# Padding three small SBUF tiles to 64 bytes, so that the tiles laid out behind them start elsewhere within 64 bytes

## The chip, the cores and the metric

The kernel runs on one core of a Trainium2 chip. The metric is the device time of one execution in microseconds. Before the change it is 2839.8 us, the median of three runs (2837.2, 2839.8 and 2843.13 us). One further execution was profiled; every row below comes from it.

## What is computed

Two blocks follow each other on 512 latent tokens of width 1024 (and 256 context tokens in the first block). All arithmetic is float32.

```python
x = ffn_sub(x, mod_lat[0:3], norm1_w, ffn1_w1, ffn1_w2)          # SwiGLU, 1024 -> 2*2816 -> 1024
s_ctx = ffn_sub(s_ctx, mod_ctx[0:3], norm1_w, ffn1_w1, ffn1_w2)
ctx_mix, lat_mix = parallel_mixer(h_ctx, h_lat, w_in, ...)       # HGRN2 and mLSTM heads
x = x + mod_lat[5] * lat_mix
x = ffn_sub(x, mod_lat[6:9], norm3_w, ffn2_w1, ffn2_w2)
# second block
y_ssm = _mamba2_mixer(...) @ w_ssm_out
y_nsa = _nsa_mixer(...) @ w_nsa_out
h = h + gate1 * ((sigmoid(hn @ w_gs) * y_ssm + sigmoid(hn @ w_ga) * y_nsa) @ w_o)
h = h + gate2 * _hier_moe(hn2, ...)                              # 32 experts, 2 per token
out = _rmsnorm(h, final_g)
```

`_hier_moe` sends each token to two of 32 experts; an expert is a SwiGLU of width 256.

## The kernel before, in words

**Dense products.** Every dense product (both FFNs, all input projections, the output projections) is done by `mm3` (lines 210 to 212). A float32 operand is split into a high and a low part of type fp32r, and three matmuls add up in PSUM: weights-high by features-high (L210), weights-high by features-low (L211), weights-low by features-high (L212). The stationary operand, which a weight load brings into the array ahead of each matmul, is a slice of 128 columns of `whi` or `wlo`; the moving operand is a slice of 512 columns (latent tokens) or 256 columns (context tokens, or half of the latent ones) of a feature tile. In one place, `proj_tok` (L555 to L557), the roles are turned round: 256 columns of `whi` or `wlo` move and 128 columns of the features are stationary. A psum tile takes 24 matmuls in a row (8 slices of the inner dimension by 3) in the projections and in the first layer of an FFN; in the second layer (`hh`, `hl` by the weights of `w2`) it takes 6 or 9. FFN 1 does latent and context tokens in turn, FFN 2 latent tokens alone.

**Feature tiles.** `lath`, `latl` (latent features, pool `hn`, used by almost every product up to 2360 us), `ctxh`, `ctxl` (context, pool `b1`), `hh`, `hl` (hidden layer of the FFN, pool `act`, opened anew for each FFN), `y0h`, `y0l`, `mh`, `mlo` (tail, pool `mo`), `y1h`, `y1l` (tail, pool `yy`). The experts read `ew` (weights, pool `ea`; here they move, as plain float32, and `xg` and `hT` are stationary), and L2176 and L2177 add each expert's rows up with `yhl` (pool `mo`) moving and `ohT` (pool `eb`) stationary, both fp32r.

**Where tiles lie.** Pools are stacked in SBUF. Those on the left are laid one behind the other in the order in which they are opened, from the low end: `cst` (constants), `hn`, `b1`, then the pools of each stage; `mo` is laid where `hn` was. Those on the right grow down from the high end: `tp` (nine tiles of 2048 bytes) and under it `wp` with `wraw`, `whi`, `wlo`. Within a pool tiles stand in the order of their first use, and each one's bytes per partition are rounded up to a multiple of 32. So a tile of four bytes takes 32, and moves all that lies behind it, in its pool and in the pools on top, by half of 64 bytes. The addresses that this gives in the program before, each as the rest after division by 64, and by 128:

| tile | role | rest by 64 | rest by 128 |
|---|---|---|---|
| `whi`, `wlo` (186,336 and on) | weights | 32 | 96 |
| `lath`, `latl` (21,504 and 37,888) | features | 0 | 0 |
| `ctxh`, `ctxl` | features | 0 | 0 |
| `hh`, `hl` of FFN 1 (125,120 and on) | features | 0 | 64 |
| `hh`, `hl` of FFN 2 (123,104 and on) | features | 32 | 96 |
| `y0h`, `y0l`, `y1h`, `y1l`, `mh`, `mlo` | features | 0 | 0 |
| `yhl` moving, `ohT` stationary | experts' sum | 0, 0 | 0, 64 |
| `ew` moving, `xg` stationary | experts | 0, 0 | 0, 0 |

Slices of a tile begin at multiples of 512 bytes further on, so every matmul of a tile has the rests of its tile.

**The three small tiles.** `eps` (L110, `setup`) holds 1e-6 for the norms and stands fourth in `cst`, ahead of everything else that is laid on the left. `inv` (L1133, `rope_tables`) holds the rope frequencies; it is allocated in pool `xq` while FFN 2 runs, and pool `act` of FFN 2 lies on top of `xq`. `frs` (L2240, `finish`) is the last tile of `mo`, and `yy`, `ea` and `eb` lie on top of `mo`.

**Order of the work.** Instructions are put in order by a scheduler at build time, with priorities that the code sets; weights come by DMA on SP's queue into `wraw` and are split by ScalarE (L191, `whi`) and VectorE (L192, `wlo`).

Of the kernel before, what the change touches and what calls it, by code (L numbers as in the profile page):

```python
# [10 lines left out]
F32 = mybir.dt.float32  # L11
# [29 lines left out]
class Kern:  # L41
# [60 lines left out]
    def setup(self):  # L102
        nc, cst = self.nc, self.cst
        self.ident = cst.tile([128, 128], F32, name="ident")
        nc.sync.dma_start(self.ident, self.i["k_ident"])
        self.ones = cst.tile([128, 128], F32, name="ones")
        nc.vector.memset(self.ones, 1.0)
        self.sel4 = cst.tile([128, 32], F32, name="sel4")
        nc.sync.dma_start(self.sel4, self.i["k_sel4"])
        self.eps = cst.tile([128, 1], F32, name="eps")  # L110
        nc.vector.memset(self.eps, 1e-6)
        self.tiny = cst.tile([128, 1], F32, name="tiny")
        nc.vector.memset(self.tiny, 7.8e-20)

# [1011 lines left out]
class Mix2:  # L1126
# [3 lines left out]
    def rope_tables(self, i, pool, cosd, sind):  # L1130

        nc = self.nc
        inv = pool.tile([128, 1], F32, name="inv")  # L1133
        nc.sync.dma_start(inv, i["k_invf"])
        pos = i["positions_2"][0]
        pf = self.tmp("posf")
        if pos.dtype == I32:
            raw = self.tmp("pos0").bitcast(I32)
            nc.sync.dma_start(raw[0:1, :], pos[None, :])
            nc.vector.tensor_copy(pf[0:1, :], raw[0:1, :])  # L1140
        else:
            p32 = pos.bitcast(I32)
            for r in range(2):
                raw = self.tmp("pos%d" % r).bitcast(I32)
                nc.sync.dma_start(raw[0:1, :], p32[r * 512:(r + 1) * 512][None, :])
                nc.vector.tensor_copy(pf[0:1, r * 256:(r + 1) * 256], raw[0:1, 0:512:2])
        p = self.pt("pb")
        nc.tensor.matmul(p, self.ones[0:1, :], pf[0:1, :], start=True, stop=True)
        ang = self.tmp("ang")
        nc.vector.tensor_scalar(ang, p, inv, None, op0=OP.mult)  # L1150
        MG = 12582912.0
        C1, C2, C3 = 6.28125, 1.9350051879882812e-03, 3.019916050561733e-07
        k = self.tmp("kk")
        nc.vector.tensor_scalar(k, ang, 1.0 / (2 * math.pi), MG, op0=OP.mult, op1=OP.add)
        nc.vector.tensor_scalar(k, k, MG, None, op0=OP.subtract)
        for c in (C1, C2, C3):
            nc.vector.scalar_tensor_tensor(ang, k, -c, ang, op0=OP.mult, op1=OP.add)

        ab = self.tmp("ab")
        nc.scalar.activation(ab, ang, AF.Abs)  # L1160
        s = self.tmp("sn")
        nc.vector.tensor_scalar(s, ab, -1.0, 3.14159274101257324, op0=OP.mult, op1=OP.add)
        nc.vector.scalar_tensor_tensor(s, s, -8.74227766e-08, ab, op0=OP.add, op1=OP.min)
        nc.scalar.activation(s, s, AF.Sin)
        sg = self.tmp("sg")
        nc.scalar.activation(sg, ang, AF.Sign)
        nc.vector.tensor_mul(s, s, sg)
        nc.sync.dma_start(sind, s)
        nc.vector.tensor_scalar(ab, ab, -1.0, math.pi / 2, op0=OP.mult, op1=OP.add)
        nc.scalar.activation(ab, ab, AF.Sin)  # L1170
        nc.sync.dma_start(cosd, ab)
# [786 lines left out]
class Moe:  # L1958
# [271 lines left out]
    def finish(self, mo, yac, yg, fg, out):  # L2230

        nc = self.nc
        ss = mo.tile([128, 4, 2], F32, name="fss")
        for c in range(4):
            for f in range(2):
                fs = slice(f * 512, f * 512 + 512)
                j = self.tmp("fj")
                nc.scalar.activation(j, yac[:, c, fs], AF.Square, accum_out=ss[:, c, f:f + 1])
                (nc.vector if f else nc.gpsimd).tensor_tensor(yg[:, c, fs], yac[:, c, fs], fg[:, fs], op=OP.mult)  # L2239
        r = mo.tile([128, 4], F32, name="frs")  # L2240
        nc.vector.tensor_add(r, ss[:, :, 0], ss[:, :, 1])
        nc.scalar.activation(r, r, AF.Ln, bias=self.eps, scale=1.0 / D)
        nc.scalar.activation(r, r, AF.Exp, scale=-0.5)
        for c in range(4):
            if c % 2:
                nc.scalar.activation(yg[:, c, :], yg[:, c, :], AF.Copy, scale=r[:, c:c + 1])
            else:
                nc.vector.tensor_scalar(yg[:, c, :], yg[:, c, :], r[:, c:c + 1], None, op0=OP.mult)
            nc.sync.dma_start(out[c * 128:(c + 1) * 128, :], yg[:, c, :])
# [326 lines left out]
```

## Time and profile before

| | us |
|---|---|
| median of three runs | 2839.8 |
| the profiled execution, its own time | 2847.28 |
| its span, first to last instruction | 2845.5 |
| TensorE matmuls busy | 2684.1 (94%) |
| TensorE weight loads busy (beside matmuls) | 2052.9 (72%) |
| VectorE, ScalarE, GpSimd busy | 1553.9, 995.2, 280.4 |

The span is what the engines took; 1.8 us lie around it. Busy time of a matmul runs from its issue to its modelled end, and matmuls overlap, so for a dense stream the distance from one start to the next tells more than the mean duration.

### The profile page before, as it was taken

What the parts mean: (1) busy time and instruction counts of PE and PEld (TensorE: products, weight loads), DVE (VectorE), ACT (ScalarE), POOL (GpSimd) and SP (SyncE); (2) the same over time, 40 slices, a digit from 0 to 9 for tenths busy, and PEclk for the clock granted to TensorE, in tenths of its full rate; (3) what the DMA queues carried; (4) which work ended last, traced back from release to release, by engine and by line L of the source; (5) the groups of instructions that cost most, each with busy time, mean ns of one, the idle gap of its engine ahead of it and who ended that gap; (6) DMA issues with size and microseconds to landing.
All of it is one profiled execution on the core that took longest, in us unless ns stands there. A gap on an engine that the chain in (4) does not pass through costs nothing. (4 is left out here: it accounts for less than half of the span.)

```text
span 2845.5 us, 40809 instructions
## 1 busy us (share of the span) xinstructions
PE 2684.1 (94%) x16161; PEld 2052.9 (72%) x16162; DVE 1553.9 (55%) x3022; ACT 995.2 (35%) x1787; POOL 280.4 (10%) x319
## 2 busy tenths in 40 slices
PE   7999999999998887999999899999999989969997
PEld 5788888888887765678788678777777767854443
DVE  6333333338367895554435756676666664454444
ACT  5211112225235663422223424555444443231112
POOL 2000000003001220100000101121122220000000
PEclk8999999999999998999999999999999999979999
DMA  7422222134333228732333433201234367269995
GB/s 261 149 89 67 59 61 66 46 97 118 94 102 103 64 83 263 260 96 82 105 95 103 135 87 95 80 13 43 78 104 119 97 195 242 74 245 377 379 378 203
DMA packets 340996, 384.66 MB, mean 135 GB/s; under 512 B 20793, under 2 KB 251581, under 8 KB 340546
## 3 DMA queue, kind: packets, MB, share of 16 engines
q1 hardware_dynamic: 338498, 373.62, 40.7%
q0 software_dynamic: 2304, 8.39, 0.8%
q8 instruction: 129, 2.11, 0.3%
q14 instruction: 65, 0.53, 0.1%
HBM read 352.33 MB, written 29.63 MB: 134 GB/s over the span
## 5 line engine op out<-in xcount | busy, mean ns | idle before, releaser
L191 ACT CAST whi<-wraw 128x1024 fp32r<-128x1024 f32 x277 | 285.9, 1042 | 756.7 <-PE pppa L211 329.3
L210 PE MATMUL pppa<-lath,whi 128*128 128x512 f32 (+4 forms) x1344 | 523.1, 390 | 19.5 <-ACT lath L1833 5.4
L211 PE MATMUL pppa<-latl,whi 128*128 128x512 f32 (+3 forms) x1344 | 519.7, 387 | 5.1 <-DVE latl L358 3.0
L212 PE MATMUL pppa<-lath,wlo 128*128 128x512 f32 (+3 forms) x1344 | 513.2, 384 | 0.0
L192 DVE TENSOR_TENSOR wlo<-wraw,whi 128x1024 fp32r<-128x1024 f32 (+1 forms) x273 | 332.4, 1224 | 252.0 <-ACT whi L191 247.4
L210 PEld LDWEIGHTS pppa<-lath,whi 128*128 128x128 f32 (+3 forms) x1344 | 253.0, 188 | 87.4 <-ACT whi L191 11.9
L211 PEld LDWEIGHTS pppa<-latl,whi 128*128 128x128 f32 (+2 forms) x1344 | 252.6, 188 | 65.4 <-DVE latl L358 5.4
L212 PEld LDWEIGHTS pppa<-lath,wlo 128*128 128x128 f32 (+2 forms) x1344 | 252.1, 188 | 55.5 <-issue 2.5
L211 PE MATMUL pppb<-hl,whi 128*128 128x512 f32 (+1 forms) x576 | 195.3, 341 | 0.0
L210 PE MATMUL pppb<-hh,whi 128*128 128x512 f32 (+1 forms) x576 | 193.1, 344 | 0.0
L212 PE MATMUL pppb<-hh,wlo 128*128 128x512 f32 (+1 forms) x576 | 191.5, 341 | 0.0
L416 DVE SCALAR_TENSOR_TENSOR xT<-pppb,sG,xT 128x512 f32<-128x512 f32 (+1 forms) x144 | 96.7, 689 | 137.7 <-PE pppb L212 137.5
L396 DVE TENSOR_TENSOR hf<-sg,pppa 128x256 f32<-128x256 f32 (+1 forms) x68 | 39.7, 584 | 234.6 <-PE pppa L212 233.3
L210 PE MATMUL pppf<-lath,whi 128*128 128x512 f32 x320 | 128.9, 403 | 5.9 <-ACT lath L1833 2.2
L210 PE MATMUL pppa<-ctxh,whi 128*128 128x256 f32 (+1 forms) x440 | 125.1, 284 | 7.9 <-DVE W L919 7.9
L211 PE MATMUL pppf<-latl,whi 128*128 128x512 f32 x320 | 128.3, 401 | 0.8 <-DVE latl L1834 0.7
L2137 PE MATMUL pppa<-ew,xg 128*64 128x512 f32 x512 | 128.3, 607 | 0.0
L212 PE MATMUL pppf<-lath,wlo 128*128 128x512 f32 x320 | 127.4, 398 | 0.6 <-DVE wlo L192 0.6
L210 PEld LDWEIGHTS pppb<-hh,whi 128*128 128x128 f32 x576 | 108.0, 188 | 27.6 <-issue 5.8
L211 PE MATMUL pppa<-ctxl,whi 128*128 128x256 f32 (+1 forms) x440 | 124.6, 283 | 0.3 <-POOL ctxl L356 0.3
L212 PE MATMUL pppa<-ctxh,wlo 128*128 128x256 f32 (+1 forms) x440 | 124.7, 284 | 0.0
L211 PEld LDWEIGHTS pppb<-hl,whi 128*128 128x128 f32 x576 | 108.4, 188 | 16.1 <-issue 3.4
(697 smaller groups left out, 4999.6 us busy)
## 6 DMA issues: line engine op xcount, KB each, us to landing
wraw<-in_ffn_w_dram SPq DMA_DIRECT2D x132, 512.0 KB, 3.9
wraw<-in_w_in_dram SPq DMA_DIRECT2D x102, 512.0 KB, 4.0
ew<-in_w_exp_gate_dram SPq DMA_DIRECT2D x64, 512.0 KB, 8.0
ew<-in_w_exp_up_dram SPq DMA_DIRECT2D x64, 512.0 KB, 4.6
ew<-in_w_exp_down_dram SPq DMA_DIRECT2D x32, 1024.0 KB, 10.6
mraw<-in_w_mod_dram SPq DMA_DIRECT2D x40, 512.0 KB, 6.5
wraw<-in_w_mod_dram SPq DMA_DIRECT2D x32, 512.0 KB, 3.9
mraw<-in_w_ada_dram SPq DMA_DIRECT2D x32, 512.0 KB, 5.8
```

What stands on the lines that cost most here:

```text
L191: nc.scalar.copy(hi[:, :n], raw[:, :n])
L192: (nc.gpsimd if pool else nc.vector).tensor_sub(lo[:, :n], raw[:, :n], hi[:, :n].bitcast(F32))
L210: nc.tensor.matmul(out, wh, xh, start=start, stop=False)
L211: nc.tensor.matmul(out, wh, xl, start=False, stop=False)
L212: nc.tensor.matmul(out, wl, xh, start=False, stop=stop)
L396: nc.vector.tensor_mul(h[:, :n], sg[:, :n], pp[1])
L416: nc.vector.scalar_tensor_tensor(x[:, o, :], p[:, :n], gate[:, o:o + 1], x[:, o, :], op0=OP.mult, op1=OP.add)
L2137: nc.tensor.matmul(ph[x * 64:x * 64 + 64, :], xg[:, k, x * 64:x * 64 + 64], wts[k // 4 * 2 + x][:, :, k % 4, :], start=(k == 0), stop=(k = ...
```

## The change

Three tiles become 64 bytes wide, and the code uses the part of them that it used before. No operand, loop or instruction is otherwise touched; the one memset of `eps` covers 16 columns in place of 1.

```diff
-        self.eps = cst.tile([128, 1], F32, name="eps")
-        nc.vector.memset(self.eps, 1e-6)
+
+        eps = cst.tile([128, 16], F32, name="eps")
+        nc.vector.memset(eps, 1e-6)
+        self.eps = eps[:, :1]
...
-        inv = pool.tile([128, 1], F32, name="inv")
+        inv = pool.tile([128, 16], F32, name="inv")[:, :1]
...
-        r = mo.tile([128, 4], F32, name="frs")
+        r = mo.tile([128, 16], F32, name="frs")[:, :4]
```

## Rows read from the trace of the kernel before

**Rows 1.** The page: span, and each engine's busy time, share and instructions
```profile
span 2845.5 us, 40809 instructions
PE 2684.1 (94%) x16161; PEld 2052.9 (72%) x16162; DVE 1553.9 (55%) x3022; ACT 995.2 (35%) x1787; POOL 280.4 (10%) x319
```
**Rows 2.** Busy time by stretch, FFN 1 and FFN 2; PEclk is the granted clock
```profile
core 0: us, PE busy (x) PEld busy (x) DVE busy (x) ACT busy (x) POOL busy (x), PEclk, DMA share, GB/s
100.00:700.00 600.00, 595.19 (x3472) 501.05 (x3467) 246.71 (x390) 146.75 (x232) 21.95 (x27) 1.00 0.26 80
1200.00:1580.00 380.00, 370.98 (x1677) 295.75 (x1676) 172.51 (x228) 105.99 (x145) 7.10 (x11) 0.99 0.33 99
```
**Rows 3.** Timeline of PE, 512 columns: `y1h` and `y1l`, first matmul and the next stream's
```profile
2384.07 0.39 PE L210 MATMUL pppa<-y1h,whi 128*128 128x512 f32 x1
...
2406.47 0.39 PE L210 MATMUL pppa<-y0h,whi 128*128 128x512 f32 x1
```
**Rows 4.** Timeline of PE, 512 columns: `hh` and `hl` of FFN 2
```profile
1284.74 0.40 PE L210 MATMUL pppb<-hh,whi 128*128 128x512 f32 x1
...
1286.36 0.39 PE L211 MATMUL pppb<-hl,whi 128*128 128x512 f32 x1
1286.59 0.39 PE L212 MATMUL pppb<-hh,wlo 128*128 128x512 f32 x1
...
1300.87 0.39 PE L212 MATMUL pppb<-hh,wlo 128*128 128x512 f32 x1
```
**Rows 5.** Timeline of PE, 512 columns: `yhl` by `ohT`
```profile
2583.66 0.39 PE L2177 MATMUL pppb<-yhl,ohT 128*128 128x512 f32 x1
...
2586.93 0.39 PE L2177 MATMUL pppb<-yhl,ohT 128*128 128x512 f32 x1
```
**Rows 6.** Timeline of PE, 256 columns: context, turned round, FFN 2
```profile
144.83 0.28 PE L210 MATMUL pppa<-ctxh,whi 128*128 128x256 f32 x1
...
150.08 0.28 PE L210 MATMUL pppa<-ctxh,whi 128*128 128x256 f32 x1
...
730.27 0.28 PE L555 MATMUL pppa<-whi,lath 128*128 128x256 f32 x1
...
730.98 0.28 PE L555 MATMUL pppa<-whi,lath 128*128 128x256 f32 x1
...
1537.36 0.28 PE L210 MATMUL pppb<-hh,whi 128*128 128x256 f32 x1
...
1538.80 0.28 PE L210 MATMUL pppb<-hh,whi 128*128 128x256 f32 x1
```
**Rows 7.** Groups by line and shape: how many matmuls; mean ns is the modelled duration
```profile
L210 PE MATMUL pppa<-lath,whi 128*128 128x512 f32 x1160 | 467.8, 404 | 16.2 <-ACT lath L1833 5.4 <-ACT lath L1105 5.0 <-ACT whi L191 4.8
L210 PE MATMUL pppf<-lath,whi 128*128 128x512 f32 x320 | 128.9, 403 | 5.9 <-ACT lath L1833 2.2 <-ACT whi L191 1.7 <-DVE mth L1852 1.1
...
L210 PE MATMUL pppa<-ctxh,whi 128*128 128x256 f32 x432 | 122.8, 284 | 7.9 <-DVE W L919 7.9
...
L555 PE MATMUL pppa<-whi,lath 128*128 128x256 f32 x192 | 54.9, 289 | 0.0
```
**Rows 8.** The same groups within 60 to 680 us: the second layer of FFN 1
```profile
L210 PE MATMUL pppb<-hh,whi 128*128 128x256 f32 x224 | 62.2, 284 | 0.0
L210 PE MATMUL pppb<-hh,whi 128*128 128x512 f32 x152 | 61.3, 403 | 0.0
```
**Rows 9.** Groups of plain float32 matmuls: in NSA, in SSD, the experts'
```profile
L2137 PE MATMUL pppa<-ew,xg 128*64 128x512 f32 x512 | 128.3, 607 | 0.0
...
L1452 PE MATMUL pppa<-PT,vt 128*64 128x128 f32 x640 | 60.3, 283 | 0.3 <-DVE PT L1434 0.3
...
L1751 PE MATMUL pppa<-W,xt 128*64 128x128 f32 x256 | 23.8, 285 | 0.0
```
**Rows 10.** DMA issues of 512 KB: KB each, median us to landing
```profile
wraw<-in_ffn_w_dram SPq DMA_DIRECT2D x132, 512.0 KB, 3.9
...
mraw<-in_w_mod_dram SPq DMA_DIRECT2D x40, 512.0 KB, 6.5
```

## The prediction

> **What bounds the kernel now.** The page comes first: TensorE is busy for 94% of the span, VectorE for 55%, ScalarE for 35% [rows 1]. [...] A modelled duration (403 ns) overlaps the next matmul, so I read the pace from the timeline, as the distance between starts.
>
> There the reader sees two paces for matmuls of the same shape. The tail's `y1h` and `y1l` take 96 matmuls of 512 columns from 2384.07 to 2406.47 us: 22.40 / 96 = 233.3 ns each [rows 3]. The second layer of FFN 2 takes 63 (21 times three) from 1286.59 to 1300.87: 14.28 / 63 = 226.7 ns [rows 4]. Both streams have a new weight load for every matmul and no idle time. What differs is where the moving tile begins: weights at rest 32 in both, `y1` at 0, `hh` of FFN 2 at 32, so that only here features and weights stand at the same place. The fast pace isn't there at once: the first seven of that stream, from 1284.74 to 1286.36, take 1.62 / 7 = 231.4 ns, and then it locks in [rows 4].
>
> At 256 columns the order is the other way round. Context products (0 against 32) take 45 matmuls in 5.25 us, 116.7 ns each; products turned round (weights moving at 32, features loaded at 0) 0.71 / 6 = 118.3; FFN 2 with both at 32 takes 12 in 1.44 us, 120.0 ns [rows 6]. Standing at the same place costs 3.3 ns there.
>
> **What the change does, part by part.** `eps` goes from 4 to 64 bytes, rounded 32 to 64: all behind it on the left moves up by 32, `lath`, `latl`, `ctxh`, `ctxl`, FFN 1's `hh` and `hl`, `mh` and `y0` among them, from rest 0 to rest 32. `whi` and `wlo` hang from the high end and stay. `inv` adds 32 under pool `act` of FFN 2, 64 in all, which keeps its `hh` at rest 32 by 64 (123,104 becomes 123,168; by 128 it goes from 96 to 32, a point I come back to). `frs` adds 32 above `mo`, so `yy`, `ea` and `eb` move by 64 and keep their rests: `y1` stays at 0 against 32. No instruction is added; the memset of `eps` has 15 columns more before the first product, where all wait for the first loads, and I price it at nothing.
>
> *512 columns.* `lath` and `latl` have 1160 + 320 matmuls on each of three lines [rows 7], 4440; FFN 1's second layer 152 on each [rows 8], 456. Together 4896, each 233.3 - 226.7 = 6.6 ns faster once locked: -32.3 us. Lock-in takes some back: seven matmuls at 231.4 in place of 226.7 are 33 ns a stream. If every 24 matmuls began anew, 4896 / 24 = 204 streams would give back 6.7 us; many run longer (63 in rows 4 alone), so I take 4.5. That leaves -27.8 us.
>
> *256 columns.* Context: 432 on each of three lines [rows 7], 1296 by 3.3 ns, +4.3 us. The products turned round: 192 on three lines [rows 7], 576 by 120.0 - 118.3, +1.0 us. FFN 1's second layer has 672 [rows 8], in short streams between the 512-column ones; I take nothing, and +2.2 us as the upper end. Smaller groups of both widths on `lath`, `y0` and `mh` have both signs and are left out.
>
> *Experts.* `xg`, stationary, moves to 32 and `ew`, moving, stays at 0; `yhl` moves to 32 against `ohT` at 0. Plain float32 matmuls don't show the place: `PT` by `vt`, both at 0, 283 ns; `W` by `xt`, both at 32, 285 [rows 9]. So nothing for `xg`. From both sides: its 512 matmuls run in pairs, and 256 times 6.6 ns is 1.7 us either way.
>
> *Transfers and other engines.* `mraw`, `xT` and the rows that the experts gather now land at rest 32. `wraw` stands there already and lands 512 KB in 3.9 us, `mraw` at 0 in 6.5 [rows 10]: nothing to pay. VectorE and ScalarE, which split the weights and make `hh` and `hl`, are busy for 246.71 and 146.75 of FFN 1's 600 us [rows 2], so matmuls 3% faster still leave them cover; next late would be the split weights, at the first matmul of a stream.
>
> *Sum.* -27.8 + 4.3 + 1.0 = -22.5 us. In the FFNs 98.6% of the time is TensorE's (966.17 of 980), so I take 22 us. The profiled execution took 2847.3 us in all, which becomes 2825; it is 7.5 us over the median of the runs, 2839.8, from which 22 us leave 2818 us.
>
> **Rivals.**
>
> *128 bytes decide, not 64.* Against the forecast stands one stream: `yhl` by `ohT`, both at rest 0 by 64, takes 3.27 / 14 = 233.6 ns [rows 5], the slow pace, though moving and stationary stand at the same place within 64. By 128 they are 64 apart, while FFN 2's fast stream has 96 and 96. If the distance counts within 128, the change takes `lath` from 0 to 32 against 96, still apart: no gain. FFN 1's `hh` goes from 64 to 96 and meets the weights, but in streams of six to nine, which end as the lock begins; FFN 2's `hh` goes from 96 to 32 and loses: 152 on three lines there too, 456 by 6.6 ns, +3.0 us. About 2842 us. For the forecast speak two things: in `yhl`'s case both are at 0, while the only fast stream has both at 32, and a start halfway into 64 bytes may be what is needed; and the stream of `yhl` is short, 15 matmuls in these rows.
>
> *Slower: the 256-column price without the 512-column gain.* If 64 bytes are enough for the pace of 120.0 ns, but 226.7 needs 128, then context and turned products pay 5.3 us, FFN 2's second layer 3.0 us, FFN 1's 256-column part up to 2.2: 2839.8 + 8 to 10, about 2849 us. It decides as soon as `ctxh` runs at 120 and `lath` stays at 233. Against it: in FFN 2 both appear together.
>
> *The place plays no part.* FFN 2's stream could be fast for another reason, for instance that one weight tile serves it and no 256-column matmul comes between. Then nothing moves: 2840 us. Against it: `y1` has no 256-column neighbours either, and is slow [rows 3, 4]. [...]
>
> **How the numbers follow.** The forecast gets 0.52, 128 bytes 0.28, no part 0.06, slower 0.14. The first is all faster: its best end has no lock-in and no 256-column price (2839.8 - 32.3 = 2807.5), its worst 6.7 us of lock-in, 7.5 us of 256-column price (2822). The second and third are within 0.2% (5.7 us, about what a measurement of this kernel can tell from no change), the fourth beyond. Faster 0.52, same 0.34, slower 0.14. The likeliest case alone ranges from 2807 to 2824; the range given, 2807 to 2845, takes in the two cases without change as well and leaves out the slower one. The predicted time is that of the likeliest, 2818.
>
> **What would show it.** In the timeline of the changed kernel, `lath` in FFN 2 should start every 226.7 to 228 ns in long streams, with some seven slower ones at each start, `ctxh` every 120, `y1` still every 233.3, and FFN 2's `hh` still every 226.7. If `lath` stays at 233 and FFN 2's `hh` falls back to 233, 128 bytes decide; if `ctxh` goes to 120 and `lath` does not follow, the slower rival. If all paces are as forecast and the time isn't, the waits for `whi` and for `hf` in the FFNs have taken the gain. Paces other than these two on `lath` would make the whole argument wrong.

## The result and the profile after

The changed kernel takes 2822.8 us (median of five runs, 2818.4 to 2827.2) where the kernel before takes 2843.1 (median of five, 2837.2 to 2847.9): ratio 0.9924, 95% interval 0.9903 to 0.9944. That is 20.3 us less by the medians. The forecast was 22 us less, and 2818 us. The total came close to the forecast; the paces it was built from did not, and most of this document is about that.

The page after: the span is 25.3 us shorter and TensorE's busy time 24.6 us, with the same number of instructions; the other engines are where they were [rows 1].

```profile
span 2820.2 us, 40809 instructions
PE 2659.5 (94%) x16161; PEld 2052.4 (73%) x16162; DVE 1552.7 (55%) x3022; ACT 994.8 (35%) x1787; POOL 276.4 (10%) x319
```

Busy time by stretch, FFN 1 and FFN 2: both stretches are as full as before, but more matmuls fit into them, 3516 for 3472 and 1745 for 1677 [rows 2] (the second stretch now also catches more of what follows FFN 2). The granted clock is the same, 1.00 and 0.99.

```profile
core 0: us, PE busy (x) PEld busy (x) DVE busy (x) ACT busy (x) POOL busy (x), PEclk, DMA share, GB/s
100.00:700.00 600.00, 595.14 (x3516) 508.60 (x3515) 250.89 (x391) 146.83 (x233) 21.92 (x27) 1.00 0.26 80
1200.00:1580.00 380.00, 371.87 (x1745) 302.56 (x1744) 181.56 (x242) 109.84 (x153) 13.78 (x19) 0.99 0.33 101
```

The timeline of TensorE, first and last rows of six streams. In order: 48 context matmuls (to the first `hh` behind them), 96 of products turned round (to the first `ctxh`), 96 later ones of the same shape, 141 on `lath` and `latl` in FFN 2, the 72 on `hh` and `hl` that follow, and 96 on `y1`.

```profile
141.27 0.28 PE L212 MATMUL pppa<-ctxh,whi 128*128 128x256 f32 x1
...
146.92 0.39 PE L212 MATMUL pppb<-hh,whi 128*128 128x512 f32 x1
...
689.37 0.28 PE L557 MATMUL pppa<-whi,lath 128*128 128x256 f32 x1
...
700.28 0.28 PE L557 MATMUL pppa<-whi,ctxh 128*128 128x256 f32 x1
...
739.79 0.28 PE L557 MATMUL pppa<-whi,lath 128*128 128x256 f32 x1
...
751.10 0.28 PE L557 MATMUL pppa<-whi,ctxh 128*128 128x256 f32 x1
...
1289.74 0.40 PE L213 MATMUL pppa<-latl,whi 128*128 128x512 f32 x1
...
1322.03 0.39 PE L212 MATMUL pppb<-hh,whi 128*128 128x512 f32 x1
...
1338.51 0.39 PE L212 MATMUL pppa<-lath,whi 128*128 128x512 f32 x1
...
2360.40 0.40 PE L212 MATMUL pppa<-y1h,whi 128*128 128x512 f32 x1
...
2382.81 0.39 PE L212 MATMUL pppa<-y0h,whi 128*128 128x512 f32 x1
```

The distance between starts, divided by the count: context 5.65 / 48 = 117.7 ns (116.7 in rows 6, not the 120 of the forecast); turned round 10.91 / 96 = 113.6 in one stream and 11.31 / 96 = 117.8 in another (118.3 in rows 6); `lath` 32.29 / 141 = **229.0**, a pace that no row of before has; `hh` of FFN 2 16.48 / 72 = 228.9 (227.2 over its whole first stream before, 16.13 / 71 from the first of rows 4 to the last); `y1` 22.41 / 96 = 233.4, unchanged [rows 3]. The same stream of `lath` before, from the same place in FFN 2:

```profile
1302.15 0.39 PE L211 MATMUL pppa<-latl,whi 128*128 128x512 f32 x1
...
1335.04 0.40 PE L210 MATMUL pppb<-hh,whi 128*128 128x512 f32 x1
```

32.89 / 141 = 233.3 ns. So one matmul on `lath` became 4.3 ns cheaper, not 6.6.

To add this up over the kernel, I take for every kind of stream the mean distance between starts (gaps over 300 ns, or 160 at 256 columns, left out) and multiply its difference to before by the number of matmuls. I call this **the account** below.

| stream (matmuls) | before, ns | after, ns | us |
|---|---|---|---|
| `lath`, 512 columns (4464) | 233.5 | 229.5 | -17.6 |
| FFN 1's `hh`, 512 columns (456) | 233.0 | 230.6 | -1.1 |
| products turned round, 256 (768, context included) | 118.3 | 115.0 | -2.5 |
| `y0` and `y1` (384) | 233.3 | 231.4 | -0.7 |
| context, 256 (1320) | 116.9 | 117.2 | +0.3 |
| FFN 2's `hh`, 512 columns (456) | 227.5 | 228.9 | +0.6 |
| smaller groups (`hh` and `lath` at 256, `mh`, `yhl`) | | | -1.1 |

Together -22.1 us, of 25.3 by the spans and 20.3 by the medians. Here nothing has to be sought beyond the matmuls' pace; the question is what sets it.

### The profile page after: what moved, and what is told of

It is laid out like the page before. It is cut to its first block, busy times and chain, and to the rows that moved or that the text cites. A ratio compares the mean times of both kernels' runs of the same rounds, so it can differ in the third digit from the quotient of the medians.

```text
span 2820.2 us, 40809 instructions
## 1 busy us (share of the span) xinstructions
PE 2659.5 (94%) x16161; PEld 2052.4 (73%) x16162; DVE 1552.7 (55%) x3022; ACT 994.8 (35%) x1787; POOL 276.4 (10%) x319
## 5 line engine op out<-in xcount | busy, mean ns | idle before, releaser
L398 DVE TENSOR_TENSOR hf<-sg,pppa 128x256 f32<-128x256 f32 (+1 forms) x68 | 39.7, 584 | 228.6 <-PE pppa L214 227.2
```

The source lines that it names most:

```text
L398: nc.vector.tensor_mul(h[:, :n], sg[:, :n], pp[1])
```

## The experiments

All places below are rests by 256, and a **distance** is how far the features stand past the weights by 256. From the addresses in front: weights 224; before, `lath`, `ctxh`, `y0`, `y1` 0 (distance 32), FFN 1's `hh` 192 (224), FFN 2's `hh` 224 (0). In the changed kernel the distance is 64 for `lath`, `ctxh` and `y0`, 0 for FFN 1's `hh`, 64 for FFN 2's and 96 for `y1`. In products turned round the weights move, so the distance counts the other way: 224 before, 192 after. Every ratio and difference is to the kernel before on the same chip, whose median was 2842.2 us beside the three kernels with another `eps`, 2845.7 beside the two with the weights moved, and 2841.9 beside the last three.

**Streams run alone.** A kernel of its own, with one stream per pair of places; 26 pairs at 512 and at 256 columns. Its inner part (`REPS` is 4):

```python
for rep in range(REPS):
    for k in range(8):
        s = slice(wo + (k % 8) * 128, wo + (k % 8) * 128 + 128)
        for q, v in enumerate((vh, vl, vh)):
            nc.tensor.matmul(p[:, :n], w[:, s], v[:, mo:mo + n],
                             start=(rep == 0 and k == 0 and q == 0), stop=(rep == REPS - 1 and k == 7 and q == 2))
```

> This kernel leaves out the whole model: it only runs streams of 96 fp32r matmuls of 512 columns, then the same of 256 columns, each matmul with a fresh weight load, nothing else beside them. The letter behind m says where the moving operand begins, the letter behind w where the weights do, as the rest after division by 256 in steps of 16 bytes (A 0, B 16, C 32, D 48, E 64, G 96, H 112, I 128, K 160, O 224). Theory 1, the distance within 128 bytes decides: at 512 columns AA, CC, EE, GG 226.7 ns a matmul, the pairs 64 apart (AE, CG, EA, GC) 229.6 as lath shows it now at 32 by 96, all pairs 32 or 96 apart 233.3; AI, GO, CK like AA, GG, CC; at 256 columns 120.0 on the diagonal and 117 elsewhere. Theory 2, it is where the moving tile begins: columns mC and mG fast (226.7 to 229.6) whatever the weights, mA and mE 233.3. Theory 3, the place plays no part: all 26 streams of a width within 0.5 ns of each other.

The timeline: the weights stand at 32 (`wC`), the features at 0, 32, 64 and 96; each row is the first of 96 matmuls, the last row the first of the next case.

```profile
97.18 0.40 PE L40 MATMUL nmAwC<-vh,w 128*128 128x512 f32 x1
...
119.57 0.40 PE L40 MATMUL nmCwC<-vh,w 128*128 128x512 f32 x1
...
141.34 0.40 PE L40 MATMUL nmEwC<-vh,w 128*128 128x512 f32 x1
...
163.74 0.40 PE L40 MATMUL nmGwC<-vh,w 128*128 128x512 f32 x1
...
185.72 0.39 PE L40 MATMUL nmAwE<-vh,w 128*128 128x512 f32 x1
```

22.39, 21.77, 22.40 and 21.98 us by 96: 233.2, 226.8, 233.3 and 229.0 ns. Beside them VectorE only copies each stream's result, 25 copies of 17.28 us in all, and busy time by stretch shows a granted clock of 1.00 with TensorE busy for 575.00 of 575 us:

```profile
11.00:586.00 575.00, 575.00 (x2485) 466.54 (x2484) 17.28 (x25) 0.00 (x0) 0.00 (x0) 1.00 0.00 1
```

So the place plays a part (theory 3 falls), it isn't where the features alone begin (theory 2 falls: `mC` is fast against `wC` and slow against `wA`, `wE` and `wG`), and the distance counts. But not by 128 as theory 1 had it (the first letter is the features' place, the second the weights'): `AI`, `CK` and `OG`, equal by 128 and 128 apart by 256, take 232.3 to 232.4 and not 226.7, and 64 past is fast (`EA`, `GC` 229) where 64 short is slow (`AE`, `CG` 233.3). By 256 every stream whose two operands begin at multiples of 32, as tiles do, fits one row (means over the second half of each stream):

| distance by 256 | 512 columns, ns | 256 columns, ns |
|---|---|---|
| 0 | 226.7 | 120.0 |
| 32 | 233.3 | 117.8 |
| 64 | 228.9 | 117.8 |
| 96 | 233.3 | 120.0 |
| 128 | 232.4 (one 233.3) | 118.7 |
| 160 | 234.2 | 118.6 |
| 192 | 233.3 | 113.3 (`AE`), 117.8 (`CG`) |
| 224 | 233.3 | 118.3 |

The changed kernel's `lath`, FFN 2's `hh` and `y1` are rows 64, 64 and 96 of this table, those of the kernel before rows 32, 0 and 32; `yhl` by `ohT` [rows 5] is row 192. Weights that begin at an odd multiple of 16 don't fit: at distance 0 `BB` has 233.3, `DD` 230.0 and `HH` 231.1, and `CD`, 16 short, has 226.7.

**eps alone.** The other two pads as in the kernel before; the edit is to the changed kernel.

```diff
-        inv = pool.tile([128, 16], F32, name="inv")[:, :1]
+        inv = pool.tile([128, 1], F32, name="inv")[:, :1]
...
-        r = mo.tile([128, 16], F32, name="frs")[:, :4]
+        r = mo.tile([128, 4], F32, name="frs")[:, :4]
```

> Only eps is widened; inv and frs stay as in the kernel before. lath, ctxh, y0, mh and FFN 1's hh stand where the change puts them, FFN 2's hh goes to 0 by 96, y1 to 32 by 96. Theory 1 (eps alone carries the gain, through lath's place): lath at 512 columns 229.6 ns, y1 229.6 in place of 233.4, FFN 2's hh 233 in place of 228.9 (456 by 4 ns, +2 us), FFN 2's 256 columns 117; about 2823 to 2826 us, ratio to the kernel before 0.992 to 0.994. Theory 2 (the gain hangs on all three pads): less than half of it is left, over 2832 us.

2826.0 us, ratio 0.9946 (0.9929 to 0.9962). `lath` 229.6 and `y1` 228.9 (distance 64), FFN 2's `hh` 233.1 (distance 32). The account gives -21.8 us where the medians give -16.2. The paces and the time are those of theory 1: `eps` carries the gain. By the account, of the other two pads, `inv` is worth 1.9 us (`hh` of FFN 2 at 64 in place of 32), and `frs` costs 1 (`y1` at 96 in place of 64).

**eps wider still.** All that the change moves by 32 moves by 64, or by 96.

```diff
-        eps = cst.tile([128, 16], F32, name="eps")
+        eps = cst.tile([128, 24], F32, name="eps")
```

> eps widened to 96 bytes in place of 64, so that all that the change moves by 32 moves by 64; inv and frs as in the change. lath, ctxh and y0 stand at 64 by 96, FFN 1's hh at 0, FFN 2's hh at 64, y1 at 96. Theory 1 (distance within 128: 32 apart is slow, from which side ever): lath 233.3 ns, ctxh 116.9, FFN 2's hh 233.3, y1 226.7 with its lock-in; 2843 us plus 2 for FFN 2's hh less 1 for y1, ratio 0.999 to 1.002. Theory 2 (any move away from the old place helps, or the moved transfers and other engines' tiles bring the gain): about as the change, 2823 us, ratio 0.992. Theory 3 (distance counted one way only, 96 minus 64 = 32 being nearer than 96 minus 0): in between, lath about 229 to 231.

2853.5 us, ratio 1.0051 (1.0033 to 1.007): slower than before. `lath` 233.6, FFN 2's `hh` 233.3, and `ctxh` goes from 116.9 to 119.9, which alone is +3.8 us; the account is +7.8 us, of 11.3 by the medians. Distance 96 has the high price in both columns of the table, 233.3 and 120.0 ns. Theory 1 had the paces of `lath` and of FFN 2's `hh` right; those of `ctxh`, of `y1` (226.7 expected, 233.3 measured, at distance 128) and the time it had wrong, since 96 and 32 are not the same distance. Theory 2, that any move helps or that moved transfers bring the gain, falls.

```diff
-        eps = cst.tile([128, 16], F32, name="eps")
+        eps = cst.tile([128, 32], F32, name="eps")
```

> eps widened to 128 bytes, so that all that the change moves by 32 moves by 96; inv and frs as in the change. lath, ctxh, y0, mh, FFN 2's hh stand at 96 by 96, the place of the weights by 128 as well as by 64; FFN 1's hh at 32, y1 at 0. Theory 1 (distance within 128; 0 apart gives the full pace at 512 columns and costs at 256): lath 226.7 to 227.5 ns (4464 by 2 to 3 ns below the change, -10 to -13 us), ctxh 120.0 in place of 117.2 (1308 by 2.8, +3.7 us), products turned round 120 in place of 115 (768 by 5, +3.8 us), lath at 256 columns 480 by 3, +1.5 us; net -2 to -5 us against the change, 2818 to 2821 us, ratio 0.991 to 0.992. [...] Theory 3 (lock-in never comes in streams of 24): lath 230 or more, 2828 to 2832 us.

2850.6 us, ratio 1.0029 (1.0014 to 1.0044). This was the test of "the same place by 64 and by 128", 96 and 96, and none of the theories had the time (only theory 3's "230 or more" fits `lath`'s pace). The timeline of the same stream on `lath`:

```profile
1304.63 0.39 PE L213 MATMUL pppa<-latl,whi 128*128 128x512 f32 x1
...
1337.53 0.40 PE L212 MATMUL pppb<-hh,whi 128*128 128x512 f32 x1
```

32.90 / 141 = 233.3 ns; other streams of it have 232.4, the mean is 232.8. By 256 features and weights are 128 apart, and 232.4 is what that row of the table has. The account is +1.1 us; what the other 7 us of the median are isn't shown.

**The weights moved, the features left.** If the distance decides, it can be had from either side. Kernel before, with one pad on the right that takes the weights down to 0:

```diff
         nc.vector.memset(self.tiny, 7.8e-20)
+        pw = self.tp.tile([128, 56], F32, name="pw")
+        nc.vector.memset(pw, 0.0)
```

> The kernel before with eps, inv and frs as they were; the weights move instead: a pad of 224 bytes among the temporaries on the right takes whi and wlo from rest 224 to rest 0 by 256, where lath, ctxh, y0, y1 and mh stand all along. Theory 1 (the distance from weights to features by 256 decides, with the paces of the streams run alone: 0 apart 226.7 and 120.0 ns, 32 apart 233.3 and 117.8, 32 short 233.3 and 118.3): lath at 512 columns 227 ns (4452 by 6.7, -30 us), y0, y1 and mh 504 by 6.7, -3.4 us; against it ctxh 120 (1302 by 3.1, +4.0), products turned round 120 (768 by 1.7, +1.3), lath at 256 columns +1.0, FFN 2's hh 233.3 in place of 227.5 (456, +2.6); FFN 1's hh 233 as before and 113 to 118 at 256 columns (-0.5 to -3.6 us). Net -25 to -28 us, ratio to the kernel before 0.990 to 0.991. Theory 2 (it is where the features themselves begin, not the distance): lath, y0 and y1 stay at 233.3, ratio 0.999 to 1.001. Theory 3 (128 bytes, as in the forecast's rival): same paces as theory 1 for lath, but FFN 2's hh at 96 by 0 and FFN 1's at 64 by 0 like lath at 96 and 64 by 0; the streams run alone speak against it.

2824.9 us, ratio 0.9928 (0.99 to 0.9955), with every feature tile where it was before. The timeline, context and `lath` streams as above:

```profile
143.76 0.28 PE L212 MATMUL pppa<-ctxh,whi 128*128 128x256 f32 x1
...
149.51 0.40 PE L212 MATMUL pppb<-hh,whi 128*128 128x512 f32 x1
...
1299.57 0.40 PE L213 MATMUL pppa<-latl,whi 128*128 128x512 f32 x1
...
1331.59 0.40 PE L212 MATMUL pppb<-hh,whi 128*128 128x512 f32 x1
```

`lath` 32.02 / 141 = 227.1, `ctxh` 5.75 / 48 = 119.8, `y1` 226.7, FFN 2's `hh` (now at distance 224) 233.3: as the table has it, for both widths. Here the forecast's own numbers appear, 6.6 ns less at 512 columns and 3 more at 256. Over the whole kernel `lath` has 227.9 (-24.7 us) and context +3.6, turned round +1.2, FFN 2's `hh` +2.7; the account is -21.4 us, near the measured 20.8. The expected 25 to 28 was too much by the start of each stream: about 300 of some 4200 gaps on `lath` are still 231 or 236 ns, nearly all among the first twelve of a stream, and behind the twelfth the mean is 226.7.

**Each stream at its best.** Three pads more than in the run before: `ctxh` at distance 64, FFN 1's `hh` at 192, FFN 2's at 0.

```diff
                     lat = [hp.tile([128, 8, L], F32R, name="lat" + x) for x in "hl"]
+                    pc = hp.tile([128, 16], F32, name="pc")
+                    self.nc.vector.memset(pc, 0.0)
...
+                ph = self.act.tile([128, 48], F32, name="ph")
+                nc.vector.memset(ph, 0.0)
...
-        inv = pool.tile([128, 1], F32, name="inv")
+        inv = pool.tile([128, 64], F32, name="inv")[:, :1]
```

> As the run before, with three pads more, so that each stream stands where the streams run alone were fastest: 64 bytes behind lath take ctxh and ctxl to 64 past the weights, 192 bytes keep FFN 1's hh at 64 short of them, inv of 256 bytes puts FFN 2's hh at the weights' own place. Theory 1: lath at 512 columns 227 ns, ctxh 117 in place of 120 (-3.7 us against the run before), context products turned round 114 to 118 (-0.5), FFN 2's hh 227.5 (-2.6) and 120 at 256 columns (+0.4); 31 to 34 us below the kernel before, ratio 0.988 to 0.989, and 10 to 14 us below the changed kernel. Theory 2 (faster matmuls now run into another wait, for split weights or loads): paces as said, ratio 0.992 or more, with idle time of TensorE in the FFNs in place of the gain.

2818.5 us, ratio 0.9902 (0.9879 to 0.9925), the lowest median of all versions. `lath` 228.0, `ctxh` 117.7, FFN 2's `hh` 226.8, FFN 1's `hh` at 256 columns 115.7 (118.6 before); the account is -27.1, the measurement -27.2 us. So no wait took the gain (theory 2 falls); the expected 31 to 34 was again too much by the start of streams.

**Streams run alone, finer.** The first kernel with weights at 224 and distances in steps of 16, and with three questions more: the stream ahead, the load's width (`cols`), and distances past 256. Two lines of it:

```python
s = slice(wo + k * 128, wo + k * 128 + cols)
...
nc.tensor.matmul(p[:cols, :n], w[:, s], v[:, mo:mo + n],
```

> This kernel leaves out the whole model, as the first one with streams alone. Weights stand at 224 by 256, as in the kernel; n and h are streams of 96 matmuls of 512 and 256 columns, with the distance of the features past the weights in bytes (0 to 240 in steps of 16); x0 to x13 are 256 columns at distances 0, 64, 0, 192, 32, 64, 32, 192, 64, 192, 128, 64, 128, 192 in turn; c64 and c32 have weight loads of 64 and 32 columns in place of 128 at distances 0, 32, 64, 128; ta to tj are streams of 24 that alternate widths; p256, p288, p512 are distances past 256 at 512 columns. Theory 1 (distance by 256 decides): n000 226.7, n032 233.3, n064 228.9, n096 233.3, n128 232.4, n160 234.2, n192 and n224 233.3; h000 120.0, h032 and h064 117.8, h128 118.7; h192 113.3 or 117.8; p256 and p512 as n000, p288 as n032; x of one distance alike up to two states at 64 and 192 that the start of the stream picks. If the extra time over the columns is what a weight load takes from the moving stream: c64 and c32 nearer to each other and to the bare columns, c32 below 225 ns at every distance and the spread between distances a quarter of that with 128. Theory 2 (the load's width plays no part, the place costs per matmul): c32 as n of the same distance. Theory 3 (absolute place): n differs from the first streams of the same distance.

At 512 columns the distances 0 to 224 in steps of 32 repeat the table: 226.7, 233.3, 228.9, 233.3, 232.4, 234.3, 233.3, 233.3. A whole 256 past is as fast as 0 (226.7 in its second half), and 288 as slow as 32 (233.3). At 256 columns 192 gives 113.3 in all five long streams, whatever ran ahead of them at that width, but 117.6 and 117.7 in two short ones behind 512 columns; 160 gives 117.3 here and 118.6 in the first kernel, 32 gives 116.7 for 117.8, so at 256 columns the distance isn't all (theory 3 in part). The widths of the loads: the rows are the first of 96 matmuls with loads of 32 columns at distance 0, and the last of them, which shares its row (x2) with the first at distance 32.

```profile
790.13 0.39 PE L43 MATMUL c32d<-vh,w 128*32 128x512 f32 x1
...
812.14 0.63 PE L43 MATMUL c32d<-vh,w 128*32 128x512 f32 x2
```

22.01 / 95 = 231.7 ns at distance 0, where loads of 128 columns give 226.7; at distance 32 the stream has 233.1, as with 128. Loads of 64 columns give 230.0 and 231.0. At distances 64 and 128 loads of 64 columns give 228.6 and 229.4, loads of 32 give 231.7 and 230.9 (128: 228.9 and 232.4). Neither theory holds: a narrower load shrinks the spread between the distances from 7 ns to some 2, but to the middle (64 columns) or the slow end (32), and the fastest of these eight streams has 228.6. What part the load has therefore stays open; a stream with fewer loads than matmuls, which would tell whether the loads are behind it at all, wasn't run.

**The features moved back by 32.** `eps` and `tiny` share a tile, all on the left falls to 224, the weights' place, with less memory than before.

```diff
-        self.eps = cst.tile([128, 1], F32, name="eps")
+        et = cst.tile([128, 2], F32, name="eps")
+        self.eps, self.tiny = et[:, :1], et[:, 1:]
         nc.vector.memset(self.eps, 1e-6)
-        self.tiny = cst.tile([128, 1], F32, name="tiny")
```

> The kernel before, but eps and tiny share one tile, so that everything behind them on the left moves back by 32: lath, ctxh, y0, y1 and mh go from 0 to 224 by 256, the place of the weights, which stay; FFN 1's hh goes to 160 (64 short of the weights), FFN 2's to 192 (32 short). Every distance is the one of the run with the weights moved, reached from the other side and with 32 bytes less of memory. Theory 1 (the distance by 256 decides): paces and time as in that run: lath 228 ns, ctxh 120, FFN 2's hh 233, 2822 to 2827 us, ratio 0.991 to 0.994. Theory 2 (the absolute place has a part too): lath's pace off 228 by over 1 ns.

2828.1 us, ratio 0.9946 (0.9927 to 0.9965). `lath` 228.0, `ctxh` 119.7, FFN 2's `hh` 233.4: the paces of the run with the weights moved, to 0.1 ns, so for them only the distance counts. The account is -21.1 us for 13.8 by the medians, and the time is 1 us above what was expected; the ratio's interval overlaps that of the run with the weights moved.

**The same, with context 64 short of the weights.**

```diff
+                    pc = hp.tile([128, 48], F32, name="pc")
+                    self.nc.vector.memset(pc, 0.0)
...
+                ph = self.act.tile([128, 16], F32, name="ph")
+                nc.vector.memset(ph, 0.0)
...
-        inv = pool.tile([128, 1], F32, name="inv")
+        inv = pool.tile([128, 32], F32, name="inv")[:, :1]
```

> As the run before, with three pads more: 192 bytes behind lath take ctxh to 64 short of the weights (160), 64 bytes keep FFN 1's hh there, inv of 128 bytes puts FFN 2's hh at the weights' place. Theory 1: the pace at 64 short, 113.3 ns in long streams run alone and 117.8 in short ones behind 512 columns, comes on ctxh as a mixture, 114.5 to 116 (1302 by 2 to 3 ns below the run with ctxh at 64 past, -2.5 to -4 us), the rest as there: 2813 to 2817 us, ratio 0.988 to 0.990. Theory 2 (in streams of 24 behind 512 columns the faster state never comes): ctxh 117.7, 2818 us, ratio 0.990.

2820.9 us, ratio 0.9914 (0.9895 to 0.9933). `ctxh` 117.5: the pace of theory 2, though the time is 3 us above its 2818 where the account has -28.2. Its streams of 48 follow `lath` at 512 columns and all take the slower of the two paces. Context products turned round follow 256-column ones; here, at distance 64, they have 113.3, where in the version with each stream at its best, at 192, they had 117.8. So 64 has the two paces as well, and which of them a stream takes isn't settled by its distance.

Nor is the stream ahead what keeps the faster pace away. In the changed kernel, with context at distance 64, 24 context streams of 20 matmuls or more follow `lath` at 512 columns without a gap: 20 take 117.8 or a little more, four take 113.3 from their first matmuls on, and none lies between. One of the four, up to the `lath` behind it:

```profile
195.46 0.28 PE L212 MATMUL pppa<-ctxh,whi 128*128 128x256 f32 x1
...
200.90 0.39 PE L212 MATMUL pppa<-lath,whi 128*128 128x512 f32 x1
```

5.44 / 48 = 113.3 ns, against 117.7 for the stream at 141.27 us shown with the result. In the version with each stream at its best, at the same distance but with weights at 0 and context at 64, none of the 24 does. What picks the pace isn't shown.

**The changed kernel again**, on the same chip.

> The changed kernel as it is, beside the two above on one chip, so that they can be set against it directly. Expected: lath 229.5 ns, ratio to the kernel before 0.991 to 0.994, and 4 to 10 us above the run with ctxh at 64 short of the weights.

2824.6 us, ratio 0.9938 (0.9917 to 0.9959), `lath` 229.6: as the first time (no edit), and 3.7 us above the run before, a little less than expected. Nine of the 24 context streams take 113.3 here, four did the first time, with the same program. The version with each stream at its best was not run beside the changed kernel; across chips its median is 4 to 6 us lower, 5 by the account. All these intervals of the ratios overlap, so that either version is faster than the changed kernel isn't shown.

By the medians six kernels come out 3.5 to 7.4 us above what the account gives them: `eps` alone, both wider ones, and the three of the last set (17.3 us gained here where the account has 22.3). The two with the weights moved agree to 0.6 us. The account leaves out waits and all work outside these streams; what the rest is, and whether the pads bring it, isn't shown.

## Why the prediction was right in its time and wrong in its terms

*What bounds the kernel.* Right: TensorE bounds the FFNs, busy after the change too for 595.14 of 600 us and 371.87 of 380, and its pace is what the change altered, by the account 22.1 of some 20 to 25 us (17 when it was measured again), and TensorE's twelve longest waits are the same ones in the profile after, the longest 8.9 us for 8.5, and none of them grew by more than 0.9 us in all. Rows 10 had `mraw` at 6.5 us and `wraw` at 3.9; after, they are 6.8 and 4.1, so moved landings cost nothing that shows.

*512 columns.* The step that failed is "features and weights stand at the same place" within 64 bytes as the condition of 226.7 ns. The fast stream of rows 4 has distance 0 by 256 as well; the one other stream read whose distance is 0 by 64, `yhl` by `ohT` [rows 5], has 192 by 256, and is slow, 233.6 ns. The change brings `lath` to distance 64, which has a pace of its own, 229.5, neither of the two that the prediction knew (by its own last sentence the argument was wrong there); so the term was -18.7 us (`lath` -17.6, FFN 1 -1.1) and not -27.8. The slow start of streams was well sized where the distance is 0: `lath`'s mean there is 1.2 ns over 226.7, 5.4 us for 4464, where 4.5 was taken.

The sentence "What differs is where the moving tile begins" said more than the trace gave, for the place isn't all in which those two streams differ: in busy time by stretch the DMA share is 0.14 during the fast `hh` stream and 0.80 during the slow one of `y1`. That the place alone is enough was shown only by the streams run alone.

```profile
core 0: us, PE busy (x) PEld busy (x) DVE busy (x) ACT busy (x) POOL busy (x), PEclk, DMA share, GB/s
1286.50:1300.10 13.60, 13.60 (x62) 11.26 (x61) 6.14 (x9) 0.35 (x1) 0.00 (x0) 1.00 0.14 40
2384.10:2406.40 22.30, 22.30 (x97) 17.94 (x96) 10.57 (x13) 5.99 (x7) 0.00 (x0) 1.00 0.80 213
```

*256 columns.* The price of +5.3 us didn't come. It belongs to distance 0 (119.7 to 120 on `ctxh` with the weights moved), and to 96 (119.9). At 64 context had +0.3 us (-0.8 when it was measured again, with more streams at the faster pace), and the products turned round gained 2.5 us, at distance 192. The two errors, 9 us too much gain and 7.5 us too much price, nearly cancelled by luck, and the smaller groups gave a little more. That the time fell within 5 us of the forecast says nothing for the mechanism.

*FFN 2's `hh` kept.* Wrong in kind, small in size: it fell from 227.5 to 228.9 (+0.6 us), since it left distance 0 for 64. The prediction had seen that by 128 it moves, and gave that to a rival.

*The experts.* `yhl` by `ohT` 233.1 before and 233.9 after, +0.2 us, as its distance went from 192 to 160; nothing, as taken.

*Rivals.* "128 bytes decide" was right that 64 aren't the measure, and wrong in its own: 96 by 128 against 96 is slow (2850.6 us). Its row, `yhl` by `ohT`, was the best hint in the trace that a wider measure counts. "The 256-column price without the 512-column gain" isn't what this change did, but it exists: moved by 64 in place of 32 (distance 96), `ctxh` pays 3 ns (119.9 for 116.9), `lath` gains nothing (233.6 for 233.5), and the kernel is slower than before by 0.5%. "The place plays no part" falls with the first streams run alone: from 226.7 to 234.2 ns with only VectorE's copies beside them. What the place changes is the pace at which matmuls with a load beside each follow one another; how it does so, these runs don't show. No fp32r stream of 512 columns here came below 226.7.

*The chances.* Faster was right. Of the cases, none was the true one as it was written: the likeliest had the time, a rival had the reason to doubt it.

## What to carry to other kernels

Where TensorE is dense and every matmul has its own weight load, look at start-to-start distances by the operands' places, by 256 bytes and not by 64 alone, as it was here. In this kernel 512 columns want features and weights at the same place (`lath` 227.9 ns there, 233.5 at 32 past), 256 columns are better 64 past or short of it (`ctxh` 117.7 and 117.5) and pay at the same place and at 96 past (119.8 and 119.9); a pad of a few words, or two small tiles that share one, is all it took, and a pad chosen by a smaller measure cost 0.5% (2853.5 us). When a prediction rests on one fast stream, write down every property in which it differs, and run short streams alone over that property before fitting tiles to it: one such kernel gave the table that three guesses at the layout had missed.

## What the runs showed of the hardware that was not expected

- Run alone, the pace of fp32r matmuls with a load each depended on the distance from weights to features by 256 bytes, and not evenly: 226.7 ns at 0, 228.9 at 64, 232.4 to 234.3 elsewhere in steps of 32 (512 columns). Distance 240, reached by a start 16 bytes short of the weights, was as fast as 0 (226.7).
- At 256 columns distances 0 and 96 were the slowest in steps of 32, 120.0 ns, and 160 has had 117.3 and 118.6. 64 and 192 have two paces, 113.3 and 117.8; alone in long streams 64 took the slow one and 192 mostly the fast one. In the model a whole stream has one or the other from its start: four context streams of 24 had 113.3 in one execution of the changed kernel and nine in another, all at distance 64.
- Weights that begin at an odd multiple of 16 bytes don't fit this: 233.3 at distance 0 with both at 16.
- Loads of 32 columns in place of 128 made the stream at distance 0 slower, 231.7 ns for 226.7, and left the one at 32 as slow as it was, 233.1.
